# A two-layer hybrid trunk: the instruction queues of VectorE, ScalarE and GpSimd follow the kernel's own planner

## The chip, the cores and the metric

One NeuronCore of a Trainium2 chip. The metric is the device time of one execution in microseconds (us): the median over runs, lower is better. The engines are PE (TensorE, with its weight loads shown as PEld), DVE (VectorE), ACT (ScalarE), POOL (GpSimd) and SP, which only issues DMAs.

## What is computed

Two layers over 512 latent tokens and 256 context tokens of width 1024. In each layer both token sets are normalised and modulated, then projected by one weight `w_in` into three branches and their gates:

```
a: gated DeltaNet, 4 heads of 128, both directions (conv of 4 taps, SiLU, l2 norm of q and k, rotary angles,
   then per block of tokens a triangular solve and a state S <- S*g + k^T u)
b: RG-LRU, 512 channels, both directions (conv, two block-diagonal products, h_t = a_t h_{t-1} + b_t)
c: neighbourhood attention, 4 heads of 128, each query sees an 8x16 window and all context keys
y = sum over branches of sigmoid(gate_i) * (branch_i @ w_branch_i);  x = x + gate * rms_norm(y @ w_out)
```

The last layer returns the latent stream alone.

## The kernel before

Activations lie channel by token. Every f32 weight and activation that feeds a big product is split into two f16 parts (`hi`, `lo`), and a product is three f16 matmuls. `w_in` comes in chunks of 128 output columns (512 KB each); `proj` (line 378) makes one chunk's 24 matmuls of 512 columns and, where the context is wanted, 24 of 256.

**The planner.** The Python program that emits the kernel is itself a small simulator, `Flow` (line 50). Each piece of work is a generator with a rank (0 first, 9 last). `product` (line 121) moves the clock `now` on by the time of a matmul; `note` (line 89) books each DVE, ACT or POOL instruction on its engine with a modelled duration, and keeps when each tile is ready; `until` (line 125) lets a piece wait until its tiles are. `run` (line 65) always resumes the waiting piece of the lowest rank, so the latency-bound pieces (preps rank 1, chains and inverses 2, `pre` 3, attention and RG-LRU cores 4) go first, and the projections (`main`, rank 9) fill PE between them. The order in which instructions are emitted is thus the planner's order.

**Whose order is used.** Only PE's queue follows it: line 31 has `ORDERED = {mybir.EngineType.PE}`, and line 1561 opens `tc.manual_schedule(engines=ORDERED)`. The queues of DVE, ACT, POOL and SP are put in order by the framework, which simulates the program with its own durations and gives each engine the first emitted instruction that is then ready. On the chip each of these queues is worked off in the order in which it was written.

**Stages.** `startup` (504) loads x, forms the modulation and the first h. In a layer, `schedule` (173) lists the projections: the DeltaNet inputs of two heads (half 0) among z gates; then k, q, v of the attention heads, under which the chunks of half 0 run; then half 1 with the fourth attention head; then the gates g of branch 2, the RG-LRU inputs xb with their gates zb, the gates of branches 0 and 1, and the output product with the next layer's h (`out_tiles`, 1405; `out_tail`, 1357).

- `gdn_prep` (969) makes one head's q, k or v: conv of four taps (`conv4`, 687: one ACT and three DVE instructions on 770 columns, tiles `cba` to `coa`), a tanh into a tile `th`, a DVE product, then transposes on PE into PSUM: `pl` holds the four latent tiles and `pc` the two of the context. For k and q, DVE multiplies `pl` by the cosines and by the sines (`rope`), ACT squares each of the six tiles for the norm (`jk`), POOL adds the two halves, `rsqrt` (271) runs eight small dependent DVE instructions (`l6y`, `l6t`, `lr`), DVE scales (`kt` or `qt`), and PE transposes back into a new `pl`, which ACT copies out.
- The tag `cbuf` has two buffers, shared by the conv inputs, `th`, `qt` and `qks` (the q-k products of a half).
- `inverse` (1161) inverts a triangular 128x128 block: `pxt`, then five rounds of `pp`, `px`, `py` on PE, each followed by a DVE or ACT instruction (`ic`, `X`, `di`, `Y`) that the next product needs. `pre` (1092) makes its input, with POOL for `gm`, `dec`, `ll`, `ktl`.
- `Weights.split` (326) turns a landed chunk `raw` into `whi` (ACT) and `wlo` (DVE). `raw` has three buffers, shared with the modulation weights `wm`, the output weights `rwo` and small tables.
- `attn_block` (839) loads its bias table of 256 KB into one buffer when the block begins. The branch `xb` of the layer loads `lw` (256 KB) and splits it before the conv.
- `rg_core` (768): per direction four `lru` products into PSUM, each with a tanh on ACT into `tr` or `ti`, then exponentials, squares and scans.

Of the kernel before, what the change touches and what calls it, by code (L numbers as in the profile page):

```python
# [17 lines left out]
P = 128  # L18
# [12 lines left out]
ORDERED = {mybir.EngineType.PE}  # L31
# [18 lines left out]
class Flow:  # L50
# [4 lines left out]
    def __init__(self):  # L55
        self.now, self.tasks = 0.0, []
        self.free, self.ready, self.used = {}, {}, {}
        self.banks, self.kept, self.wire = [None] * 5, set(), 0.0
# [30 lines left out]
    def note(self, eng, op, args, kw):  # L89
# [3 lines left out]
        start = max([self.free.get(eng, 0.0)] + [self.ready.get(x.name, 0.0) for x in ins])  # L93
        if eng == "act":
            us = n / 1200.0 + 0.09 + 0.09 * sum(isinstance(kw.get(x), bass.AP) for x in ("scale", "bias", "accum_out"))
        elif eng == "pool":
            us = n / 510.0 + 0.1 if op == "tensor_tensor" else n / 1100.0 + 0.12
# [6 lines left out]
        for x in ins:  # L104
            self.used[x.name] = max(self.used.get(x.name, 0.0), end)
        for x in (aps[0], kw.get("accum_out")):
            if x is not None:
                self.ready[x.name] = end + LAT

# [6 lines left out]
    def fetched(self, dst):  # L116

        self.wire = max(self.wire, self.now) + 4 * math.prod(dst.shape) / 357e3
        self.ready[dst.name] = self.wire + FETCH

    def product(self, dst, us):
        self.now += us
        self.ready[dst.name] = self.now + LAT

# [24 lines left out]
    def drop(self, *tiles):  # L149
        self.kept.difference_update(t.name for t in tiles)  # L150

# [47 lines left out]
def build(tc, A, out):  # L199
# [25 lines left out]
    def mm(dst, lhsT, rhs, **kw):  # L225
        n = math.prod(rhs.shape[1:])
        nc.tensor.matmul(dst, lhsT, rhs, **kw)  # L227
        fl.product(dst, max(n, 64) * (4 if rhs.dtype == F32 else 1) / 2400.0)

    def tp(dst, src_, idt):  # L230
        nc.tensor.transpose(dst, src_, idt)  # L231
        fl.product(dst, P * (2 if src_.dtype == F32 else 1) / 2400.0)

    def pair_t(name, wide=True):

        return (plat.tile([P, SEQ], F32, tag="lat", name=name),
                pctx.tile([P, CTX], F32, tag="ctx", name=name + "c") if wide else None)
# [18 lines left out]

    def load_consts():
# [4 lines left out]
        t = wp.tile([P, 5, P], F32, tag="raw", name="tri", bufs=3)  # L262
# [4 lines left out]
    def put_consts(t):  # L267
        V.tensor_copy(C["tri"], t)
        C["cum"], C["sgt"], C["ones"] = C["tri"][:, 0:2], C["tri"][:, 2:4], C["tri"][:, 4]
# [36 lines left out]
    class Weights:  # L306
# [11 lines left out]
        def load(self):  # L318
            if self.seq:
                src_, nk, key = self.seq.pop(0)  # L320
                raw = wp.tile([P, nk, P], F32, tag="raw", name="raw", bufs=3)
                nc.sync.dma_start(raw, src_)
                fl.fetched(raw)
                self.raw.append((raw, nk, key))

        def split(self, pool_=None):
            if self.raw:
                raw, nk, key = self.raw.pop(0)
                kw = {"bufs": 3 if pool_.name == "n0" else 1} if pool_ else {}
# [10 lines left out]
                for k in range(0, nk, step):  # L340
# [3 lines left out]
                    V.scalar_tensor_tensor(lo[:, ks], raw[:, ks], SW, hi[:, ks], op0=OP.mult, op1=OP.subtract)  # L344
                ready.append(True)
# [7 lines left out]
        def ahead(self):  # L353
            self.load()
# [23 lines left out]
    def proj(nk, xs, wide, nm, key, shared=False):  # L378

        w = yield from W.take(key)  # L380
        if shared:
            yield from fl.room(1 + wide)
            o = (pst(nm, [P, SEQ], keep=True), pst(nm + "c", [P, CTX], keep=True) if wide else None)
        else:
            o = pair_t(nm, wide)
        yield from seg(o[0], 0, w, range(nk), nk, xs, 0, SEQ, True)
        if wide:
            yield from seg(o[1], SEQ, w, range(nk), nk, xs, SEQ, NT)
        return o
# [7 lines left out]
    def mod_rows(l, part, fin, load):  # L397
# [5 lines left out]
        for k in range(KD):  # L403
# [5 lines left out]
            fl.product(pm, 0.43)  # L409
# [40 lines left out]
    def wload(l, part, k):  # L450
        raw = wp.tile([P, 2, 512], F32, tag="raw", name="wm", bufs=3)
        nc.sync.dma_start(raw, A["w_mod"][l, part, k])
        return raw

    def gate_rows(l, pp, out_, rowt):
# [4 lines left out]
        def fin(pm):  # L460
# [3 lines left out]
            selg = wp.tile([P, 2, 2, P], F32, tag="raw", name="selg", bufs=3)  # L464
            nc.sync.dma_start(selg, A["selg"])
            g = A["g_post"]
            gp = wp.tile([P, D], F32, tag="raw", name="gp", bufs=3)
# [1205 lines left out]
```

## Time and profile before

| | |
|---|---|
| median of 3 runs | 1741.05 us (1738.36 to 1744.34) |
| the profiled execution's own time | 1741.55 us |
| its span, first to last instruction | 1739.8 us |
| PE busy | 1635.1 us (94%), 11452 matmuls |
| DVE busy | 1168.1 us (67%) |
| ACT busy | 861.1 us (49%) |
| POOL busy | 351.8 us (20%) |
| DMA, mean | 80 GB/s |

Start and end of an instruction are taken from the engine; a matmul's end is modelled, so that overlapping matmuls count as busy once and a short wait can hide under the end of the one before. A wait is idle time of an engine that ended with another engine's signal.

### The profile page before, as it was taken

Reading aid. Unit: us, or ns where it says so; the run is one execution under the profiler, and the core shown is the slowest. Engines: PE = TensorE matmul, PEld = TensorE weight load, DVE = VectorE, ACT = ScalarE, POOL = GpSimd, SP = SyncE. Lnnn points to the kernel's source line nnn. Section 1 sums busy time; section 2 is a strip of 40 time slices with the busy share of each in tenths; the row PEclk is TensorE's granted clock in tenths of the full one; section 3 lists DMA queues with packets and bytes.
Section 4 is the critical chain, followed back from the end, with each engine's and each line's share of the span. In section 5 each row is a group of like instructions: output and inputs, shape, how many; then the busy total and the mean of one; then the engine's idle time right before and its main releaser. Section 6 shows DMA issues by size and latency. Waiting matters only on the chain. (4 is left out here: it accounts for less than half of the span.)

```text
span 1739.8 us, 30312 instructions
## 1 busy us (share of the span) xinstructions
PE 1635.1 (94%) x11452; PEld 1027.8 (59%) x11452; DVE 1168.1 (67%) x2752; ACT 861.1 (49%) x2050; POOL 351.8 (20%) x506
## 2 busy tenths in 40 slices
PE   5999999999999999899999888899999999999998
PEld 4556767766676555455664455577756665544443
DVE  6668777766777556655435756888666888677553
ACT  4445656455545347542432334666454655657341
POOL 0113311002321001231111212323012431012321
PEclk9999999999999999999999999999999999999999
DMA  9211111211222331243432112111121112324432
GB/s 358 59 50 50 44 32 37 67 61 43 86 62 74 122 103 43 79 133 99 134 96 93 36 37 61 43 38 44 55 67 55 44 50 68 122 91 151 139 116 73
DMA packets 48386, 139.79 MB, mean 80 GB/s; under 512 B 8048, under 2 KB 8688, under 8 KB 48240
## 3 DMA queue, kind: packets, MB, share of 16 engines
q1 hardware_dynamic: 48240, 137.86, 24.7%
q8 instruction: 90, 1.47, 0.3%
q14 instruction: 56, 0.46, 0.1%
HBM read 133.64 MB, written 4.19 MB: 79 GB/s over the span
## 5 line engine op out<-in xcount | busy, mean ns | idle before, releaser
L227 PEld LDWEIGHTS <-whi_g 128*128 128x128 f16 x1152 | 109.4, 98 | 88.3 <-issue 11.4
L164 POOL TENSOR_TENSOR gm<-trir,gst 128x256 fp32r<-128x256 f32 x96 | 67.3, 708 | 267.8 <-PE pd L227 261.6
L227 PE MATMUL 1_g<-h,whi_g 128*128 128x512 f16 x384 | 119.2, 383 | 0.2 <-ACT mt L164 0.2
L227 PE MATMUL 0_g<-h,whi_g 128*128 128x512 f16 x384 | 116.6, 379 | 0.0
L227 PE MATMUL py<-wo,mg 128*128 128x512 f16 x480 | 104.9, 379 | 0.0
L227 PEld LDWEIGHTS <-whi_a 128*128 128x128 f16 x704 | 69.5, 99 | 49.2 <-issue 7.8
L164 ACT ACTIVATE X<-px 128x256 f16<-128x256 f32 x181 | 67.6, 382 | 50.4 <-PE px L227 46.1
L164 DVE SCALAR_TENSOR_TENSOR wlo_g<-raw,whi_g 128x512 f16<-128x512 f32 x96 | 68.8, 735 | 33.7 <-ACT whi_g L164 32.5
L164 DVE TENSOR_TENSOR ic<-pp,lmc 128x128 f16<-128x128 f32 x240 | 66.4, 284 | 29.0 <-PE pp L227 26.3
L164 ACT ACTIVATE di<-py 64x128 f16<-64x128 f32 x240 | 63.6, 269 | 44.2 <-PE py L227 24.4
L227 PEld LDWEIGHTS <-whi_b 128*128 128x128 f16 x576 | 54.9, 98 | 45.2 <-issue 10.3
L227 PEld LDWEIGHTS <-wlo_g 128*128 128x128 f16 x576 | 56.4, 98 | 39.4 <-DVE wlo_g L164 0.7
L227 PEld LDWEIGHTS <-mg 128*128 128x128 f16 x480 | 47.0, 98 | 55.1
L164 DVE SCALAR_TENSOR_TENSOR coa<-cba,cva,coa 128x770 f32<-128x770 f32 (+1 forms) x72 | 76.6, 1064 | 4.0 <-ACT coa L164 2.5
L164 ACT ACTIVATE whi_g<-raw 128x512 f16<-128x512 f32 x96 | 58.2, 623 | 37.7 <-DMA raw<-in_w_in 14.9
L227 PE MATMUL 1_g<-h,wlo_g 128*128 128x512 f16 x192 | 73.3, 382 | 0.3 <-DVE wlo_g L164 0.3
L227 PE MATMUL 0_g<-h,wlo_g 128*128 128x512 f16 x192 | 72.8, 379 | 0.0
L227 PEld LDWEIGHTS <-di 128*128 128x128 f16 x480 | 39.5, 98 | 39.0 <-DVE di L164 11.0
L227 PE MATMUL pp<-X,ld 128*128 128x64 f16 x480 | 51.6, 193 | 10.1 <-DVE X L164 4.2
L164 DVE SCALAR_TENSOR_TENSOR wlo_b<-raw,whi_b 128x512 f16<-128x512 f32 x48 | 43.9, 914 | 23.4 <-ACT whi_b L164 22.8
L227 PE MATMUL py<-ident,X 128*128 128x128 f16 x384 | 50.7, 220 | 6.1 <-ACT X L164 3.6
L164 POOL TENSOR_TENSOR mt<-mg,mt 128x768 f32<-128x768 f32 (+1 forms) x16 | 28.9, 1804 | 121.3 <-DVE mt L164 103.3
(658 smaller groups left out, 4745.2 us busy)
## 6 DMA issues: line engine op xcount, KB each, us to landing
raw<-in_w_in SPq DMA_DIRECT2D x128, 512.0 KB, 3.6
wm<-in_w_mod SPq DMA_DIRECT2D x48, 512.0 KB, 4.2
raw<-in_w_branch SPq DMA_DIRECT2D x48, 256.0 KB, 2.7
rwo<-in_w_out SPq DMA_DIRECT2D x16, 512.0 KB, 4.0
xt<-in_xin SPq DMA_DIRECT2D x12, 512.0 KB, 5.0
bias<-in_rpb SPq DMA_DIRECT2D x24, 256.0 KB, 2.7
lw<-in_lru_w SPq DMA_DIRECT2D x8, 256.0 KB, 3.6
x<-xo SPq DMA_DIRECT2D x4, 512.0 KB, 2.9
```

The lines of the kernel that those rows point to most:

```text
L164: return real(*args, **kw)
L227: nc.tensor.matmul(dst, lhsT, rhs, **kw)
```

## The change

All four compute engines are queued in the emitted order, and the planner's model and the emitting pieces are altered with it. The diff has about 660 lines; its core:

```diff
-ORDERED = {mybir.EngineType.PE}
+ORDERED = {mybir.EngineType.PE, mybir.EngineType.DVE, mybir.EngineType.Activation, mybir.EngineType.Pool}
...
     def note(self, eng, op, args, kw):
-        start = max([self.free.get(eng, 0.0)] + [self.ready.get(x.name, 0.0) for x in ins])
+        start = max([self.free.get(eng, 0.0)] + [self.ready.get(x.name, 0.0)
+                                                  - (LAT / 2 if self.near.get(x.name) == eng else 0.0) for x in ins])
+        for x in ins:
+            if x.space == PSUM and self.touch.get(x.name, (eng,))[0] != eng:
+                start = max(start, self.touch[x.name][1] + LAT)
...
-            us = n / 510.0 + 0.1 if op == "tensor_tensor" else n / 1100.0 + 0.12
+            us = (n / 510.0 + 0.1 if n < 512 else n / 375.0) if op == "tensor_tensor" else n / 1000.0 + 0.12
...
-        fl.product(dst, max(n, 64) * (4 if rhs.dtype == F32 else 1) / 2400.0)
+        fl.product(dst, max(n, 70) * 4 / 2400.0 + 0.02 if rhs.dtype == F32 else max(n / 2400.0 + 0.004, 0.035))
...
+    def slot(self):
+        return len(self.ring) < 3 or self.ring[-3] in self.spent
+    def freed(self, *names):
+        for n in names:
+            if n not in self.spent:
+                yield lambda: n in self.spent
+            yield self.used.get(n, 0.0) - self.now
...
         def split(self, pool_=None):
+                if not pool_:
+                    yield fl.until(raw)
...
-            fetch_x(range(TT))
             load_first()
+            fl.fetched(cc)
+            fetch_x(range(TT))
...
         def rg_core(...):
+            yield lambda: sum(xfree) == j
...
+            yield fl.until(lwr)
+            S.activation(lw[0], lwr, AF.Copy, scale=SW)
+            yield fl.until(lw[0])
+            V.scalar_tensor_tensor(lw[1], lwr, SW, lw[0], op0=OP.mult, op1=OP.subtract)
...
+        def load_bias(pp):
+            if tables:
+                hd, i = tables.pop(0)
+                t = pp.tile([P, 512], F32, tag="bias", name="bias", bufs=2)
+                nc.sync.dma_start(t, A["rpb"][l, hd, :, i, :])
+                fl.fetched(t)
+                biases.append(t)
...
         def gdn_prep(...):
-            th = gp.tile([P, NT + 8], F32, tag="cbuf", name="th", bufs=2)
-            S.activation(th[:, :n], c[:, :n], AF.Tanh)
-            V.scalar_tensor_tensor(c[:, :n], th[:, :n], 1.0, c[:, :n], op0=OP.add, op1=OP.mult)
+            S.activation(b[:, :n], c[:, :n], AF.Tanh)
+            V.scalar_tensor_tensor(c[:, :n], b[:, :n], 1.0, c[:, :n], op0=OP.add, op1=OP.mult)
+            cbufs.remove(b.name)
...
-            pl = pst("pl", [P, LT, P], keep=True)
-            pc = pst("pc", [P, 2, P], keep=True) if wide else None
+            banks = [pst(f"pl{i}", [P, cut, P], keep=True) for i in range(2)]
...
-            V.tensor_tensor(dst[:, :LT, :], pl, C["cos"], OP.mult)
-            V.tensor_tensor(tmp ..., pl ..., C["sin"] ..., OP.mult)
-            for t, off in tiles:
-                S.activation(jk, pl[:, t, :] if t < LT else pc[:, t - LT, :], AF.Square, accum_out=ss[:, t:t + 1])
+            for i in (1, 0):
+                for t in range(i * cut, (i + 1) * cut):
+                    S.activation(jk, banks[i][:, t % cut, :], AF.Square, accum_out=ss[:, t:t + 1])
+            for i in range(2):
+                V.tensor_tensor(dst[:, ts, :], src_, C["cos"][:, ts, :], OP.mult)
+                V.tensor_tensor(tmp[:, ts, :] ..., src_ ..., C["sin"][:, ts, :] ..., OP.mult)
...
         def gdn_front(...):
+            yield lambda: len(cbufs) < 2
             b = conv_in(gp, o, "a", 2)
+            cbufs.append(b.name)
```

`near` is the engine that wrote a tile, `touch` the engine that last read a PSUM tile and when. `slot` makes a weight chunk wait for a buffer of the `raw` ring, `freed` a projection for its PSUM tile; `cbufs` counts the users of `cbuf`; `qks` takes its two buffers one by one, the second only when all six preps of the half are spawned and a buffer is free. The first two bias tables are loaded with the first k projection, the next ones each when a block has read its own, into two buffers instead of one; `lw` has two buffers and is loaded one projection earlier. `cut` is three for six tiles and two for four: tiles 0 to 2 go to one PSUM bank, 3 to 5 to the other.

## Rows read from the trace of the kernel before

**Rows 1.** Busy time by stage: stretch, its length, PE, PEld, DVE, ACT, POOL, clock, DMA.

```profile
0.00:43.50 43.50, 24.06 (x197) 17.53 (x197) 26.34 (x87) 21.73 (x48) 3.89 (x9) 0.92 0.94 358
43.50:609.00 565.50, 540.68 (x4357) 379.12 (x4356) 406.67 (x1089) 291.30 (x810) 109.92 (x206) 0.99 0.20 61
609.00:957.00 348.00, 339.44 (x1974) 192.45 (x1973) 187.36 (x272) 145.54 (x228) 62.92 (x35) 0.98 0.30 97
957.00:1044.00 87.00, 74.82 (x521) 42.70 (x519) 55.12 (x162) 28.84 (x70) 20.67 (x38) 0.94 0.11 36
1044.00:1479.00 435.00, 407.13 (x3199) 279.83 (x3200) 338.69 (x915) 248.17 (x701) 104.62 (x185) 0.99 0.17 53
1479.00:1690.00 211.00, 207.52 (x1023) 97.57 (x1022) 135.81 (x175) 119.75 (x177) 43.44 (x29) 1.00 0.40 128
1690.00:1739.80 49.80, 41.40 (x192) 18.59 (x190) 18.15 (x54) 5.80 (x17) 6.33 (x5) 0.96 0.19 64
```

**Rows 2.** Waits of PE, whole span: whom it waited for, us in total, times, longest.

```profile
PE pl L231 <- DVE kt L164: 9.2, 5, 3.7
...
PE xTp L231 <- DVE sq L164: 6.6, 1, 6.6
PE lru L227 <- ACT tr L164: 5.1, 1, 5.1
...
PE pl L231 <- DVE qt L164: 4.1, 3, 2.7
```

**Rows 3.** Busy time in three stretches at a lower granted clock, columns as in rows 1.

```profile
87.14:90.55 3.41, 3.10 (x11) 1.93 (x12) 1.81 (x3) 0.87 (x2) 0.73 (x1) 0.50 0.19 34
...
715.20:722.00 6.80, 4.08 (x12) 1.70 (x12) 3.28 (x5) 5.24 (x9) 0.00 (x0) 0.50 0.17 61
...
1094.10:1097.50 3.40, 3.40 (x16) 1.76 (x16) 3.04 (x6) 0.77 (x2) 1.90 (x3) 0.50 0.53 154
```

**Rows 4.** Timeline of DVE and PE, a k prep of the second layer.

```profile
1031.85 0.16 DVE L164 TENSOR_SCALAR lss<-lss 128x6 f32<-128x6 f32 x1
...
1034.42 1.22 DVE L164 SCALAR_TENSOR_TENSOR wlo_z<-raw,whi_z 128x1024 f16<-128x1024 f32 x1
...
1038.80 0.68 DVE L164 TENSOR_TENSOR kt<-kt,lr 128x512 f32<-128x512 f32 x1
...
1039.54 0.90 PE L231 MATMUL pl<-ident,kt 128*128 128x128 f32 x3 [3.58 <-DVE kt L164]
```

**Rows 5.** Timeline, the first inverses of the second layer.

```profile
1090.85 0.29 DVE L164 TENSOR_TENSOR Y<-lh,lm 128x256 f16<-128x256 f16 x1 [1.39 <-ACT lh L164]
...
1091.74 1.70 DVE L164 SCALAR_TENSOR_TENSOR wlo_v<-raw,whi_v 128x512 f16<-128x512 f32 x2
...
1093.36 0.58 DVE L164 COPY X<-pxt 64x256 f16<-64x256 f16 x2
...
1094.00 0.26 PE L227 MATMUL pp<-X,ld 128*128 128x64 f16 x2 [3.43 <-DVE X L164]
```

**Rows 6.** Timeline of ACT and PE, an RG-LRU core of the first layer.

```profile
715.87 0.63 ACT L164 ACTIVATE whi_g<-raw 128x512 f16<-128x512 f32 x1 [4.54 <-DMA raw<-in_w_in]
...
717.91 0.37 PE L227 MATMUL lru<-xh,lw 128*128 128x256 f16 x1 [5.13 <-ACT tr L164]
```

**Rows 7.** Timeline of the start: one of three small loads of SP, then DVE.

```profile
4.61 0.49 SPq L250 DMA_DIRECT2D ident<-in_ident  x1
...
14.56 0.17 DVE L164 TENSOR_TENSOR xss<-xss 128x4 f32<-128x4 f32 x1 [2.14 <-ACT jk L164]
...
19.12 2.73 DVE L164 TENSOR_SCALAR xt<-xt,xr 128x1024 f32<-128x1024 f32 x4
```

**Rows 8.** Groups: the hop after `pp`, the conv taps and a POOL add (ns min/median/max).

```profile
L164 DVE TENSOR_TENSOR ic<-pp,lmc 128x128 f16<-128x128 f32 x240 | 66.4, 284 | 29.0 <-PE pp L227 26.3
...
L164 DVE SCALAR_TENSOR_TENSOR coa<-cba,cva,coa x72: 733/1021/1959, 64.0 to 1344.5; 128x770 f32<-128x770 f32 x60, 128x512 f32<-128x512 f32 x12
...
L164 POOL TENSOR_TENSOR kt<-kt,rope x8: 1270/1676/2036, 76.5 to 1283.5; 128x512 f32<-128x512 f32 x8
```

More of the change, by code (lines that the diff above doesn't have):

```diff
@@ L56, in __init__ @@
         self.now, self.tasks = 0.0, []
-        self.free, self.ready, self.used = {}, {}, {}
-        self.banks, self.kept, self.wire = [None] * 5, set(), 0.0
+        self.free, self.ready, self.used, self.near = {}, {}, {}, {}
+        self.banks, self.kept, self.wire, self.ring = [None] * 5, set(), 0.0, []
+        self.spent, self.touch, self.sp = set(), {}, 0.0
     def spawn(self, gen, rank, delay=0.0):
@@ L105, in note @@
             self.used[x.name] = max(self.used.get(x.name, 0.0), end)
+            if x.space == PSUM:
+                self.touch[x.name] = (eng, end)
         for x in (aps[0], kw.get("accum_out")):
@@ L382, in proj @@
             yield from fl.room(1 + wide)
-            o = (pst(nm, [P, SEQ], keep=True), pst(nm + "c", [P, CTX], keep=True) if wide else None)
+            lat, ctx = pst(nm, [P, SEQ], keep=True), pst(nm + "c", [P, CTX], keep=True) if wide else None
         else:
-            o = pair_t(nm, wide)
-        yield from seg(o[0], 0, w, range(nk), nk, xs, 0, SEQ, True)
+            yield from fl.freed(*lats[-2:-1])
+            lat, ctx = lat_t(nm), None
+        yield from seg(lat, 0, w, range(nk), nk, xs, 0, SEQ, True)
         if wide:
-            yield from seg(o[1], SEQ, w, range(nk), nk, xs, SEQ, NT)
-        return o
+            if not shared:
+                yield from fl.freed(*ctxs[-1:])
+                ctx = ctx_t(nm)
+            yield from seg(ctx, SEQ, w, range(nk), nk, xs, SEQ, NT)
+        return lat, ctx
     def both(o):
@@ L635, in lru_rates @@
     def lru_rates():
+        yield fl.until(lam)
         V.tensor_scalar(lam, lam, -1.0, None, op0=OP.mult)
@@ L1008, in gdn_prep @@
+            for i in range(2):
+                ts = slice(i * cut, min((i + 1) * cut, LT))
+                src_ = banks[i][:, :ts.stop - ts.start, :]
+                V.tensor_tensor(dst[:, ts, :], src_, C["cos"][:, ts, :], OP.mult)
+                V.tensor_tensor(tmp[:, ts, :].rearrange(sw, two=2, q=32), src_.rearrange(sw, two=2, q=32)[:, :, ::-1, :],
+                                C["sin"][:, ts, :].rearrange(sw, two=2, q=32), OP.mult)
             yield fl.until(tmp)
@@ L1065, in finish @@
                 yield ended(*chains)
+                for t in half["qks"]:
+                    cbufs.remove(t.name)
                 r = small.tile([P, 2, TT], F32, tag="orr", name="orr")
@@ L1118, in pre @@
                             yield lambda: half["used"] >= len(half["kk"]) - 3
+                        if want(s):
+                            slot = half["slots"]
+                            half["slots"] += 1
+                            i = slot // 3
+                            yield lambda: (i < len(half["qks"]) or
+                                           len(cbufs) < 2 and (i == 0 or len(half["preps"]) == 6))
                         yield from fl.room(2)
@@ L1136, in pre @@
                         if want(s):
-                            if "qks" not in half:
-                                half["qks"] = [gp.tile([P, 3, 2, P], F32, tag="cbuf", name="qks", bufs=2)
-                                               for _ in range(2)]
-                            qk = half["qk"][t_] = half["qks"][t_ // 3][:, t_ % 3]
+                            if i == len(half["qks"]):
+                                half["qks"].append(gp.tile([P, 3, 2, P], F32, tag="cbuf", name="qks", bufs=2))
+                                cbufs.append(half["qks"][i].name)
+                            qk = half["qk"][t_] = half["qks"][i][:, slot % 3]
                             S.activation(qk, pqk, AF.Copy)
@@ L1414, in out_tiles @@
                 else:
-                    py = [plat.tile([P, 512], F32, tag="lat", name=f"py{hf}") for hf in range(2)]
+                    yield from fl.freed(*lats[-2:])
+                    py = [lat_t(f"py{hf}") for hf in range(2)]
                 xt = pp.tile([P, D], F32, tag="xt", name="xt", bufs=2)
@@ L1504, in layer @@
                                  o[0].rearrange("p (r n c) -> p r n c", n=4, r=8), AF.Copy, scale=UN * ATT)
+                    fl.drop(*[p for p, _ in both(o)])
                 elif kind == "v":
@@ L1522, in layer @@
                         S.activation(t[:, sl], p, AF.Tanh, scale=0.5 * UN)
+                    fl.drop(*[p for p, _ in both(o)])
                     next(side, None)
```

163 lines of the change are left out of this document (113 added, 50 removed).

## The prediction

> **What bounds the kernel now.** I read the busy time by stage first, since an average hides where PE is full. PE is busy for 540.68 of 565.50 us in the first layer's DeltaNet and attention stage, for 407.13 of 435.00 in the second layer's, for 339.44 of 348.00 between them, and for 24.06 of 43.50 at the start [rows 1]. Its idle time is therefore 19.4 us at the start, 24.8 and 27.9 in the two DeltaNet stages, 8.6 in the first layer's dense part, 12.2 where the layers meet, 3.5 in the second layer's dense part and 8.4 at the end: 104.8 us in all, and nothing that reorders queues can save more than that and what the clock gives back. PE bounds the kernel; the question is only what its waits are made of.
>
> The waits of PE come next. The named ones are k and q preps (9.2 us in 5 waits and 4.1 in 3), one wait of 6.6 for `sq` where the layers meet and one of 5.1 for `tr` in an RG-LRU core [rows 2]. The rest is many short waits in the inverses.
>
> The timelines then say whether a wait is latency or a queue. In the k prep the norm is summed at 1031.85 and `kt` is scaled at 1038.80: 7.0 us for ten small DVE instructions of some 0.16 us, because a `wlo_z` of 1.22 us, conv taps and a softplus stand between them in DVE's queue; PE then waits 3.58 us [rows 4]. In the inverses DVE sat 1.39 us before `Y`, then ran 1.70 us of weight splitting, and only then the copy `X` for which PE waited 3.43 us [rows 5]. In the RG-LRU core ACT sat 4.54 us before a weight split whose chunk had not landed, with the tanh that frees a PSUM bank behind it, and PE waited 5.13 us [rows 6]. All three are the same thing: an instruction that PE needs stands in a queue behind one that is not yet ready or not urgent. The framework ordered these queues by its own simulated times, PE by the planner's, and the two disagree. That is what the change removes.
>
> **The change part by part.** The sum is made against the profiled execution's 1741.55 us, which is 0.5 us above the median of the runs and 1.75 above its span.
>
> *Start.* Three small loads are now issued ahead of x, at some 0.49 us each [rows 7]: x and the squares come 1.5 us later. Against that, the ten small instructions from 14.56 to 19.12 [rows 7] would take about 10 x 0.2 = 2.0 us in a run instead of 4.56: 2.5 us earlier. Net -1.0; ends +1.5 and -2.5.
>
> *k and q preps.* With the norm's instructions in a run the prep of rows 4 is 7.0 - 2.7 = 4.3 us shorter (2.0 for the ten, 0.7 for the scaling), more than the 3.58 that PE waited. The two banks add two DVE instructions to each of 16 preps (about 0.15 us of fixed cost each), and let ACT's squares run beside the DVE reads instead of behind them; both are small beside 4.3. I take 12 of the 13.3 us [rows 2]; ends 0 and 13.3. The cover of the prep is the projection behind it; when a prep is no longer late, the next thing late is its own POOL add.
>
> *Short waits in the inverses, chains and attention.* The two stages hold 52.7 us of idle time [rows 1], 39.4 without the preps' 13.3. Part of it is pure latency (PE to DVE to PE, one `ic` is 284 ns [rows 8]), which no order removes but which the planner can fill with projections; part is the queueing of rows 5. No row splits them. The ends are 0 and 39.4; I take 22, a little over half, since the long ones that I opened are queueing.
>
> *Clock.* After three of the long waits (the longest for `kt`, 3.7 us [rows 2], and those of rows 4 and 5) the granted clock is 0.50, which is 1.2 GHz, for 3.4 us each; PE was busy 3.10 and 3.40 of them in the first and last [rows 3], so each costs about 1.7 us. If the waits go, so do these: -4 of 5; ends 0 and 5.
>
> *RG-LRU.* The split now waits in the planner for its chunk to land, so the tanh goes first: -5.1, and the lowered clock behind it with 4.08 us of PE [rows 3] gives back 2.0. I take -6; ends 0 and -7.
>
> *Where the layers meet.* Idle 12.2 us [rows 1]. The norm chains get shorter, but each now holds DVE for its whole length while DVE also makes h. I take 0, ends +6 and -6 (the `sq` wait of rows 2).
>
> *Biases, `lw`, `cbuf`.* 24 bias loads and 8 of `lw` are issued earlier on SP; DMA is at 0.17 to 0.20 in those stages [rows 1], so they meet nothing. The new wait for a free `cbuf` stands in `main`, so the projections queue behind it; tanh in place takes one user off, and I take 0. Its ends: nothing gained, and a loss of 8 q preps at the mean q wait of 1.4 us [rows 2], 11. SP stays in the framework's order.
>
> *The end* (8.4 us idle) and the dense parts keep their work: 0.
>
> Sum: 1.0 + 12 + 22 + 4 + 6 = 45, so 1741.55 - 45 = **1696.5**, and I say 1696.
>
> **The rivals.**
>
> *Only the long queueing waits go.* If the short waits are latency that the planner already fills as well as it can, their 22 us stay: 1741.55 - 23 = 1718. For it: ahead of `ic` DVE stood idle for 26.3 us until `pp` came [rows 8], and there the hop was prompt. Against it: rows 5. Chance 0.20.
>
> *The shared port.* A POOL add of one size takes 1.27 to 2.04 us and a conv tap 0.73 to 1.96 [rows 8]: something holds one while the other runs. The planner books POOL and DVE as if they were independent, so its order may set more of them side by side. In the two stages POOL is busy 214.5 us, and DVE 745 of 1000.5, so three quarters would already meet by chance; the last quarter is 54 us of DVE, and if half of that reached PE, 27: 1696 + 27 = 1723. Chance 0.08. The Trainium skill, "SBUF — State Buffer", section "Who interferes with whom", states such a rule: a VectorE instruction with two SBUF inputs and a GpSimd instruction that reads SBUF exclude each other for the whole instruction. By that rule the spread of rows 8 is blocking, and the trace agrees with it; the numbers above stand without it.
>
> *Slower: the strict queue holds up the hops.* The planner queues by readiness, not by urgency. A conv tap of 1.02 us (median) emitted just before an `ic` [rows 8] now stays before it on the chip, where the framework could take the `ic` first. The place is the 240 `ic` hops. If one in three waits out a whole tap, 80 x 1.02 = 82 us are added; the gains outside the hops are 23, and a third of the 82 is covered by projections: 1741.55 - 23 + 54 = 1773. It turns the sign when more than 23 / 1.02 = 23 hops of 240, one in ten, are held up uncovered. Against it: the framework's queue has these taps and splits ahead of urgent copies today (rows 4, 5), and the planner's PE order is made with the very same queue in mind. Chance 0.15.
>
> *No change.* The planner's model is off by as much as the framework's, and waits move without shrinking: 1741. Chance 0.07.
>
> **How the numbers follow.** Forecast 0.50, the rivals 0.20, 0.08, 0.15 and 0.07. About 0.3% (5 us) is what a measurement of this kernel can tell from no change. Faster: 0.50 + 0.20 + 0.08 = 0.78; same 0.07; slower 0.15. The low end: taking every term at its better end gives 2.5 + 13.3 + 39.4 + 5 + 7 + 6 = 73, 1668; since modelled matmul ends hide part of each wait, I go to 1660. The high end takes in the no-change case and the start of the slower one, 1744, and leaves out the bulk of the latter. The forecast's own range is 1668 to 1712.
>
> **What would show it.** Right: PE idle in the two DeltaNet stages falls from 52.7 to about 18 us; the waits of `pl` on `kt` and `qt` are nearly gone; the norm's ten DVE instructions stand in a run; no ACT wait for a landing with a tanh behind it; the clock at 87 and 1094 stays at 2.4 GHz; PE busy hardly moves. Wrong: `ic`, `X` or `di` named as the releaser of more PE waits than now, PE waiting for `cba` behind the new gate, longer POOL adds and conv taps, or a wider gap where the layers meet.

## The result, and the profile after

The change made the kernel slower: 1760.99 us (median of 4, 1757.16 to 1763.67) against 1742.69 us of the kernel before in the same session, a ratio of 1.0104 with a 95% interval of 1.0089 to 1.0119. Its profiled execution has a span of 1759.4 us, 19.6 above that of before. (One run of `e5_qt_elsewhere` and two of `e10_pe_split_first`, further down, were disturbed and are left out of their numbers.)

Busy time of the engines over the whole span, before and then after:

```profile
PE 1635.1 (94%) x11452; PEld 1027.8 (59%) x11452; DVE 1168.1 (67%) x2752; ACT 861.1 (49%) x2050; POOL 351.8 (20%) x506
```

```profile
PE 1647.0 (94%) x11452; PEld 1030.7 (59%) x11452; DVE 1190.2 (68%) x2784; ACT 858.1 (49%) x2050; POOL 350.6 (20%) x506
```

Two things are to be read from this pair. PE has the same 11452 matmuls and is busy 11.9 us longer, most of it by a lower clock. The granted clock is 0.979 in the mean, 0.987 before: it stands at 0.50, which is 1.2 GHz, in 15 stretches of 77.0 us together, before in 9 of 47.0. PE is busy for 52.7 and 33.5 us of them, and half the difference, 9.6 us, is an estimate of what that costs. And PE's idle time, span less busy, went from 104.7 to 112.4 us, 7.7 more. The two make the 19.6. DVE too is busy 22.1 us longer, for only 32 more instructions.

Busy time by stage after the change, to be held against [rows 1] (the work stands some 20 us later towards the end, so the last stretch is longer):

```profile
0.00:43.50 43.50, 23.30 (x178) 15.92 (x179) 25.43 (x81) 22.56 (x49) 3.77 (x8) 0.96 0.93 357
43.50:609.00 565.50, 543.81 (x4375) 382.66 (x4374) 400.96 (x1098) 290.22 (x812) 106.49 (x200) 0.99 0.20 60
609.00:957.00 348.00, 345.74 (x2012) 195.80 (x2010) 201.73 (x296) 145.26 (x236) 67.21 (x42) 0.99 0.31 97
957.00:1044.00 87.00, 70.27 (x488) 39.59 (x487) 55.86 (x147) 27.42 (x68) 16.17 (x25) 0.90 0.13 43
1044.00:1479.00 435.00, 405.96 (x3178) 278.31 (x3177) 341.46 (x934) 245.50 (x690) 108.36 (x197) 0.98 0.17 51
1479.00:1690.00 211.00, 197.23 (x950) 91.08 (x949) 136.14 (x165) 114.75 (x168) 37.90 (x26) 0.98 0.39 125
```

PE is fuller in the first layer (543.81 and 345.74 us against 540.68 and 339.44), and emptier from 957 us on: where the layers meet, and in the second layer's dense part, 13.8 us idle against 3.5.

Fixed stretches of time blur what belongs to one piece of work. So here are the lengths between landmarks, the first matmul of a named tile in each trace. The two openings hold the first k and q preparations of a layer; between `q` and `xb` lie the inverses, chains and attention. The last three columns are experiments told below: the change without its gate for q (`e5`), with three faults mended (`e11`), and that with DVE, ACT and POOL free again (`e16`).

| from, to (us) | forecast | before | after | `e5` | `e11` | `e16` |
|---|---|---|---|---|---|---|
| start to `f` | -1 | 33.4 | 32.7 | 32.8 | 31.9 | 33.2 |
| `f` to `0_q` (opening, layer 1) | preps -12 in both | 114.1 | 128.6 | 113.0 | 112.7 | 106.8 |
| `0_q` to `0_xb` | short waits -22 in both layers | 479.0 | 465.2 | 471.8 | 470.9 | 475.6 |
| `0_xb` to output product | -6 | 289.2 | 282.1 | 282.0 | 279.1 | 281.6 |
| to `1_a` (layers meet) | 0 | 101.8 | 104.7 | 104.4 | 105.8 | 102.5 |
| `1_a` to `1_q` (opening, layer 2) | as above | 70.4 | 90.7 | 72.8 | 70.4 | 68.4 |
| `1_q` to `1_xb` | as above | 395.1 | 382.5 | 388.2 | 389.0 | 388.3 |
| `1_xb` to output product | 0 | 206.8 | 222.6 | 223.8 | 213.8 | 208.8 |
| end | 0 | 50.0 | 50.3 | 50.0 | 50.3 | 50.0 |

The loss lies in three places above all: 14.5 and 20.3 us in the openings, 15.8 in the second layer's dense part. Where the layers meet 2.9 more are lost, at the end 0.3; the rest gained.

The waits of PE after the change (whom it waited for; us, times, longest), against [rows 2]:

```profile
PE pl L262 <- DVE qt L195: 14.4, 2, 7.7
PE xTp L262 <- DVE sq L195: 9.7, 1, 9.7
PE pm L467 <- DMA wm<-in_w_mod: 8.5, 5, 2.7
PE pd L258 <- POOL gm L195: 5.6, 11, 1.9
PE 1_a_q L258 <- DVE wlo_a L195: 4.9, 1, 4.9
PE 1_g L258 <- ACT whi_g L195: 4.4, 2, 2.2
PE 1_a_v L258 <- DVE wlo_a L195: 4.4, 2, 2.5
PE pxt L262 <- DVE Y L195: 4.3, 9, 1.2
...
PE 1_g L258 <- DVE wlo_g L195: 3.0, 3, 1.6
PE lru L258 <- ACT tr L195: 2.3, 1, 2.3
...
PE pl L262 <- DVE kt L195: 0.7, 2, 0.4
```

The k preps did what was forecast, 9.2 us to 0.7. The q preps did the opposite, 4.1 to 14.4, in two waits only. And new names stand in the list: `wlo_a`, `whi_g` and `wlo_g`, the two halves of a weight split. Three others grew: the landings of the modulation weights `wm` (2.9 before), and in the inverses POOL's `gm` and DVE's `Y` (1.0 and 1.1 before).

The second of the two q waits, in the timeline of all engines (the first is its twin, 6.75 us at 125.02):

```profile
1062.09 0.27 PE L258 MATMUL 1_a_v_0c<-h,wlo_a 128*128 128x256 f16 x1
...
1062.29 0.28 ACT L195 ACTIVATE jk<-pl 128x128 f16<-128x128 f32 x1 [1.77 <-PE pl L262]
...
1063.90 0.42 DVE L195 TENSOR_TENSOR qt<-pl,cos 128x256 f32<-128x256 f32 x1 [2.66 <-ACT jk L195]
...
1065.48 1.61 POOL L195 TENSOR_TENSOR qt<-qt,rope 128x512 f32<-128x512 f32 x1 [16.73 <-DVE rope L195]
1065.89 1.23 DVE L195 TENSOR_SCALAR lss<-lss 128x4 f32<-128x4 f32 x1
...
1068.55 0.16 DVE L195 SCALAR_TENSOR_TENSOR lr<-l4t,l4y 128x4 f32<-128x4 f32 x1
...
1069.29 0.68 DVE L195 TENSOR_TENSOR qt<-qt,lr 128x512 f32<-128x512 f32 x1
...
1070.03 1.12 PE L262 MATMUL pl<-ident,qt 128*128 128x128 f32 x4 [7.66 <-DVE qt L195]
1070.93 1.06 PE L258 MATMUL 1_z<-h,whi_z 128*128 128x512 f16 x2
```

The preparation is not late. Its norm stands in a run, 1065.89 to 1068.71, as forecast. What is missing is cover: between the last `1_a_v` product and the transposes of `qt` PE's queue holds nothing, and `1_z`, which needs no part of q, comes only after them.

### The profile page after: what moved, and what is told of

It reads as the page before. It is cut to its first block, busy times and chain, and to the rows that moved or that the text cites. A ratio compares the mean times of both kernels' runs of the same rounds, so it can differ in the third digit from the quotient of the medians.

```text
span 1759.4 us, 30281 instructions
## 1 busy us (share of the span) xinstructions
PE 1647.0 (94%) x11452; PEld 1030.7 (59%) x11452; DVE 1190.2 (68%) x2784; ACT 858.1 (49%) x2050; POOL 350.6 (20%) x506
## 5 line engine op out<-in xcount | busy, mean ns | idle before, releaser
L195 ACT ACTIVATE di<-py 64x128 f16<-64x128 f32 x255 | 68.5, 271 | 53.9 <-PE py L258 22.7
L195 DVE SCALAR_TENSOR_TENSOR wlo_g<-raw,whi_g 128x512 f16<-128x512 f32 x96 | 87.2, 933 | 7.0 <-ACT whi_g L195 7.0
L195 ACT ACTIVATE X<-px 128x256 f16<-128x256 f32 x164 | 60.8, 381 | 40.3 <-PE px L258 37.6
L195 DVE SCALAR_TENSOR_TENSOR wlo_b<-raw,whi_b 128x512 f16<-128x512 f32 x48 | 39.6, 825 | 51.9 <-ACT whi_b L195 51.8
L258 PE MATMUL 0_g<-h,wlo_g 128*128 128x512 f16 x192 | 72.8, 379 | 0.0
L195 POOL TENSOR_SCALAR_AFFINE_SELECT dec<-dec 128x256 f32<-128x256 f32 x48 | 22.7, 480 | 223.4 <-ACT dec L195 214.4
L195 ACT ACTIVATE whi_g<-raw 128x512 f16<-128x512 f32 x96 | 56.8, 623 | 20.3 <-DMA raw<-in_w_in 20.2
L195 POOL TENSOR_TENSOR ix<-ix,zz 128x1536 f32<-128x1536 f32 x8 | 27.6, 3449 | 176.0 <-ACT zz L195 176.0
```

The lines of the kernel that those rows point to most:

```text
L195: return real(*args, **kw)
```

## The experiments

**The queues one by one.** The four kernels differ from the change in the set of ordered queues only:

```diff
-ORDERED = {PE, DVE, Activation, Pool}
+ORDERED = {PE}                       # e1_pe_only
+ORDERED = {PE, Activation, Pool}     # e2_dve_free
+ORDERED = {PE, DVE}                  # e3_pe_dve
+ORDERED = {PE, DVE, Pool}            # e4_act_free
```

`e1_pe_only`:

> The changed kernel with one line put back: only PE follows the planner's order, DVE, ACT and POOL are ordered by the framework again; the new planner model, gates, banks and early biases stay. Theory A (the strict queues cost, the rest of the change gains): well under 1760, at or below the kernel before, 1720 to 1743, with the waits of PE for wlo_a, qt and sq shorter. Rival B (the planner's new model and gates cost, by another PE order): 1755 or more, as with the queues. Rival C (the two add up): about 1750.

`e2_dve_free`:

> The changed kernel with DVE alone ordered by the framework; PE, ACT and POOL follow the planner. Theory A in the form that DVE's queue is the one that costs: as fast as with PE alone ordered, within 5 us. Rival (ACT's queue costs, tanh and copies behind a wait for PE): no faster than 1755.

`e3_pe_dve`:

> The changed kernel with PE and DVE in the planner's order, ACT and POOL by the framework. If DVE's queue costs: 1755 to 1765, like the change. If ACT's or POOL's queue costs: like PE alone, 1720 to 1743.

`e4_act_free`:

> The changed kernel with ACT alone ordered by the framework; PE, DVE and POOL follow the planner. If ACT's queue costs (it stood 8.4 us behind a transposed copy with a tanh behind that): 1745 or less. If DVE's queue costs: 1755 to 1765.

Measured: 1746.99 us (ratio to before 1.0022, 1.0010 to 1.0033), 1759.27 (1.0087), 1773.44 (1.0174) and 1780.66 (1.0211, 1.0196 to 1.0226). Freeing all three queues gives back 14 us, and the kernel still isn't faster than before, nearest to the third expectation; freeing one or two of them gives 2 us or costs 12 and 20. `e3_pe_dve` and `e4_act_free` lie above every range expected, and why is not shown. The change missed the forecast by 64 us, so the larger part of that lies outside the new queues, and an order of half the queues is no way between.

**The gate on `cbuf`.** A q preparation no longer takes a `cbuf`, its rotated tile goes to `oa`, which isn't in use yet:

```diff
             else:
-                yield lambda: len(cbufs) < 2
-                dst = gp.tile([P, TT, P], F32, tag="cbuf", name="qt", bufs=2)
-                cbufs.append(dst.name)
+                dst = half["oa"][:, hl]
...
-            if which == "q":
-                cbufs.remove(dst.name)
```

> The changed kernel with the rotated q of a prep written into the half's output tile, which is idle until the chains run, instead of the shared conv buffers; it no longer counts against the gate that holds back the next projection. Theory A (in the opening of a layer PE waits for qt because the gate keeps the projections from being queued ahead of its transposes): the waits of pl on qt, 14.4 us in 2, fall below 4, and the time by 8 to 20 us, to 1741 to 1753. Rival B (qt is late by DVE's and ACT's strict queues alone, the gate only names it): the waits move to another tile of the prep and the time stays at 1756 to 1763.

Measured: 1740.92 us, ratio 0.9983 (0.9970 to 0.9996), 20 us faster than the change. Both openings are back at 113.0 and 72.8 us; of the 33.5 us that they gain, 12.3 are lost again between `q` and `xb`, since side work that the long openings had done is now done there (30 and 28 matmuls move). Of the 20.6 us between the two profiled runs 9.0 are idle time of PE (112.4 to 103.4), and 11.6 are busy time for the same matmuls (1647.0 to 1635.4). PE's wait for q, which was expected to fall below 4:

```profile
PE pl L262 <- DVE oa L195: 8.2, 5, 3.6
```

Is it the gate or the buffer? The next kernel puts the tile in `oa` too, but still counts it as a holder of a `cbuf`:

```diff
+                yield lambda: len(cbufs) < 2
                 dst = half["oa"][:, hl]
+                cbufs.append(f"qt{hl}")
```

> The change as it is, with q's rotated tile in `oa` as in the run that put it elsewhere (1740.9), but with the planner still counting q as a holder of a `cbuf` and still gating on it, though no buffer is taken. Theory 1: the cost of some 20 us is the gate itself, by which the planner holds the main path's next projections and q's own rotation until a buffer is counted free: this kernel stays at 1757 to 1763, with PE's wait of `pl` for q's tile near the 14.4 us of the change. Rival: the cost is the buffer, that is the hardware wait for the tile's earlier reader; then the kernel goes with the run that put q elsewhere: 1739 to 1744.

Measured: 1755.92 us, ratio 1.0070 (1.0052 to 1.0087), with the wait back:

```profile
PE pl L262 <- DVE oa L195: 20.4, 6, 7.8
```

It is the gate, for 15 of the 20 us: PE's idle time is back, 114.9 us, and what is still missing lies in its busy time, 1638.2 against 1647.0 in the change. No instruction waits for a buffer here; the planner, told that both are held until q's transposes are done, holds `main` in front of the next conv input, and so plans no projection before them. PE obeys the plan. The edit brings back two gates, q's own and that of the conv input; that the second one drains PE is read from the program and the timeline, and the two were not separated. (The time is 1.1 us under the range expected.)

The same edit on the kernel before, which has no gate:

> The kernel before, with one edit: q's rotated tile lies in its half's `oa` instead of one of the two `cbuf` buffers. Nothing else of the change is in it. Theory 1, what the first four runs suggest: the gate that the change adds is its dear part, and the change without gate and with only the tensor engine queued in order (1725.7) gains 17 us over before by its other parts. Then this edit alone changes the kernel before little: it had no gate, and its q preparations cost it 4.1 us of waits in three cases; 1738 to 1745. Rival: two `cbuf` buffers for th, q and the conv inputs are what binds in both kernels, and the whole gain belongs to the third place for q: then this kernel comes to 1726 to 1732 and the change's other parts are worth nothing. The opening from the last product of the modulation to the end of layer 1's last q (114.1 us before, 110.0 with the tensor engine alone in order and q elsewhere) would then be 110 or less here.

Measured: 1745.91 us, ratio 1.0007 (0.9996 to 1.0018). The place of the tile is worth nothing by itself. And the edit of `e5` with only PE ordered, `ORDERED = {PE}`:

> PE alone in the planner's order, as in the first experiment (1747), with q in the output tile. Theory A (the gate costs with either queue order): 1727 to 1741, below the kernel before. Rival B: 1744 to 1750, as without the edit.

Measured: 1725.74 us, ratio 0.9904 (0.9883 to 0.9924), 21 us under `e1_pe_only`. The gate costs the same, 20 or 21 us, in either order.

**The rank of the weight split.** In the change the second layer's dense part waits for `whi_g`. The timeline of ACT and PE there:

```profile
1669.74 1.06 ACT L195 ACTIVATE wo<-rwo 128x1024 f16<-128x1024 f32 x1 [4.25 <-DMA rwo<-in_w_out]
1670.70 1.13 ACT L195 ACTIVATE whi_g<-raw 128x512 f16<-128x512 f32 x2
...
1671.37 0.60 PE L258 MATMUL 1_g<-h,whi_g 128*128 128x512 f16 x2 [2.16 <-ACT whi_g L195]
```

ACT stood 4.25 us before a split of the output weights whose chunk had not landed, and `whi_g`, for which PE waited, stood behind it: the situation of [rows 6], now made by the planner, which gives weight splits rank 7, the last before `main`'s 9. The edit:

```diff
-            fl.spawn(self.split(), 7, 0.3)
+            fl.spawn(self.split(), 0, 0.3)
```

> The changed kernel with the splitting of landed weight chunks at rank 0 instead of 7. Theory A (in a strict queue work of the lowest rank comes last whenever there is a burst, and PE then waits for its weights): the waits for wlo_a, wlo_g, wlo_b, whi_g (some 20 us) fall to under 8 and those for wm landings (8.5 us) shrink since the ring turns faster; 1740 to 1753. Rival B (the splits now hold up the hops of the inverses): those waits go but others in the inverses come, 1757 to 1770.

> Both edits, q in the output tile and splits first. If the two causes are separate: the sum of the two gains, 1722 to 1745. If they are one (a late prep by whichever way): no better than the better of the two.

Measured: alone 1747.82 us, ratio 1.0032 (1.0019 to 1.0045), 13 us faster than the change; with the tile in `oa` 1730.88, ratio 0.9940 (0.9920 to 0.9960), 10 faster than `e5_qt_elsewhere`. The two gains add, but for 3 us. The dense part falls from 222.6 to 213.0 and 214.0, and PE's waits for `whi_g` and `wlo_g` are gone from the list; those for `wlo_a` in the openings stay (11.2 us in the change, 11.0 with the edit), so that the sum under 8 that was expected is missed. The rest of the dense part's loss, 6 to 7 us, goes with another wait: PE waits there for landings of `wm`, 1.1 us before, 6.9 in the change and 7.1 with the edit, which was expected to shorten these waits. Why `wm` lands late is not shown. With free queues the rank should be worth nothing:

> Only the tensor engine's queue in the planner's order, q's rotated tile in `oa`, no gate for it, and the task that splits a weight at the planner's first rank instead of its last. Theory 1: the split's rank matters only where the vector engine works strictly in the planner's order, since a free queue there is ordered by what is ready; then the rank adds nothing here: 1722 to 1729. Rival: the rank matters because it sets where the split stands in the program in either case; then the 10 to 13 us of the strict kernel appear again: 1712 to 1716, the last dense part of layer 2 shorter by 5 or more.

Measured: 1722.81 and 1723.22 us, ratio 0.9876 (0.9856 to 0.9895) beside 0.9904 without the edit; the intervals overlap, so no more than a few us, as expected.

**The softplus in one run.** At the second opening of the changed kernel, DVE and PE:

```profile
1027.02 1.66 DVE L195 SCALAR_TENSOR_TENSOR spp<-spp,spq 128x48 f32<-128x48 f32 x7
...
1027.99 0.59 PE L258 MATMUL 1_a_q<-h,whi_a 128*128 128x512 f16 x2
...
1031.60 0.68 DVE L195 TENSOR_TENSOR kt<-kt,lr 128x512 f32<-128x512 f32 x1
1032.20 1.22 DVE L195 SCALAR_TENSOR_TENSOR wlo_a<-raw,whi_a 128x1024 f16<-128x1024 f32 x1
...
1033.48 0.61 PE L258 MATMUL 1_a_q<-h,wlo_a 128*128 128x512 f16 x1 [4.89 <-DVE wlo_a L195]
```

A task that issues its softplus without handing back to the planner puts all of it into the queue at once; `wlo_a` waits behind steps that nobody is waiting for. On top of `e7_both`:

```diff
         V.reciprocal(s, s)
+        yield fl.until(s)
         V.tensor_tensor(s, s, w, OP.mult)
...
         for k in (15, 13, 11, 9, 7, 5, 3):
+            yield fl.until(p)
             V.scalar_tensor_tensor(p, p, 1.0 / k, q, op0=OP.add, op1=OP.mult)
```

> All four queues in order, q's rotated tile in `oa`, split at the first rank (1730.9), and in the softplus of the decays the planner is asked after each of some ten small vector steps instead of none, so that other work can stand between them. Theory: the run of some twenty small vector steps stands in front of wlo_a in the strict queue, and the two waits of PE for wlo_a at the opening of layer 2 (4.9 and part of 6.4 us) come from it; spread, 1721 to 1727, with the 4.9 us wait of 1_a_q for wlo_a under 1.5. Rival: PE's waits for wlo_a come from the raw buffer being filled late or from ACT's half of the split, and the burst only fills the vector engine's slack: 1729 to 1733 with the same wait.

Measured: 1723.86 us, ratio 0.9880 (0.9865 to 0.9896), 7 faster than `e7_both`, and the wait of `1_a_q` is gone from the list; that of `1_a_v`, of which a part was expected to go too, stays (6.4 and 6.8 us). This is the change with three faults mended: 20 us under before. Then the three queues free again, `ORDERED = {PE}`:

> The strict kernel with all three edits (q in `oa`, split at the first rank, softplus spread; 1723.9) with the vector, scalar and pool queues free again. If the strict queues themselves, freed of the three faults, give what the prediction took from them (22 us of short waits), this kernel is 15 us or more slower than that: 1739 or more. If a queue in the planner's order is worth nothing beside one that takes what is ready, as the run with two edits suggests (1722.8), it comes to 1720 to 1726.

Measured: 1717.89 us, ratio 0.9860 (0.9842 to 0.9879), under both ranges expected, the fastest kernel of all and 6 us under the strict one. So over the whole kernel the strict order of DVE, ACT and POOL is worth nothing here, even with its faults mended.

By stretches it is worth something, and loses more. Four pairs of kernels differ in these three queues alone: the change and `e1`, `e5` and `e8`, `e7` and `e10`, `e11` and `e16`. In each pair the strict kernel is shorter from `0_q` to `0_xb` (by 4.7 to 10.7 us) and from there to the output product (2.4 to 4.5), and longer in the openings (2.0 to 5.8 and 1.9 to 10.2), where the layers meet (1.7 to 4.0) and in the second layer's dense part (5.0 to 13.2). Each of these is one profiled run.

The softplus edit also gains with the queues free: by the medians `e16` is 5 us under `e10`, which lacks it (the intervals overlap), though `1_a_q` doesn't wait for `wlo_a` in `e10`. How much of its 7 us in the strict kernel is the burst in DVE's queue, and how much another order of PE, is open.

In `e16` PE is busy 1631.4 us of 1715.2, so idle for 83.8 against 104.7 before:

```profile
PE xTp L262 <- DVE sq L195: 6.6, 1, 6.6
PE pl L262 <- DVE kt L195: 6.0, 4, 2.5
...
PE pl L262 <- DVE oa L195: 3.0, 3, 1.7
```

**Where the gain comes from.** The two banks put back to one of 512 and one of 256, in `e10_pe_split_first`:

> Only the tensor engine's queue in order, q in `oa`, split at the first rank (1722.8), and the transposed tiles of a preparation back in one bank of 512 and one of 256, with the rope products ahead of the squares, as before the change. What is left of the change are the planner's durations and landings, the ring of raw buffers, the biases and the lru weights ahead. Theory A, the prediction's step for the preparations (12 us): the two banks shorten the path from transposes to rotated tile; undone, 1731 to 1737, PE's waits of `pl` for kt and oa back at 10 or more. Theory B: the gain of 21 us over before lies in the planner's better knowledge, which places PE's own order, and the banks are worth little: 1720 to 1727.

Measured: 1732.58 us, ratio 0.9946 (0.9924 to 0.9967): the banks, with the order of reads that goes with them, are worth 10 us there, and the waits of `pl` for kt and oa come to 13.5 us (7.1 with them). What else the change has (durations, landings, the ring, early loads), together with q in `oa` and the split first, holds this kernel 11 us under before; it was not taken apart. The banks alone on the kernel before:

> The kernel before with one part of the change alone: a preparation's transposed tiles in two banks of equal halves, the squares of the second bank first, the rope products after them. Theory A (the banks carry the preparations' 12 us): 1731 to 1736, PE's waits of `pl` for kt and qt, 13.3 us before, at 4 or less. Theory B (the gain needs the planner's knowledge): 1741 to 1748.

Measured: 1767.52 us, ratio 1.0142 (1.0122 to 1.0162): the same edit costs 24 us, which neither theory had. Waits of PE, and the k prep that answers to [rows 4]:

```profile
PE pl L231 <- DVE kt L164: 15.2, 5, 5.9
...
PE pl L231 <- DVE qt L164: 7.4, 3, 4.1
```

```profile
1039.84 0.26 ACT L164 ACTIVATE jk<-pl 128x128 f16<-128x128 f32 x1
...
1042.36 0.23 DVE L164 TENSOR_TENSOR kt<-pl,cos 128x128 f32<-128x128 f32 x1
...
1045.13 0.17 DVE L164 TENSOR_SCALAR lss<-lss 128x6 f32<-128x6 f32 x1
...
1053.18 0.68 DVE L164 TENSOR_TENSOR kt<-kt,lr 128x512 f32<-128x512 f32 x1
...
1053.91 1.11 PE L231 MATMUL pl<-ident,kt 128*128 128x128 f32 x4 [5.05 <-DVE kt L164]
```

The products of the rotation now come after the squares of their bank, 2.5 us after the first square, with other work of ACT between the squares. The old planner knows nothing of that, thinks both run at once, and puts the transposes into PE's order too early. The planner's new rule, that a bank has one reading engine at a time, is three lines of the change:

```diff
+        for x in ins:
+            if x.space == PSUM and self.touch.get(x.name, (eng,))[0] != eng:
+                start = max(start, self.touch[x.name][1] + LAT)
```

Added to the banks on the kernel before, and taken from the fastest kernel:

> The kernel before with the two banks alone (1767.5, 24 us slower than before) and one piece of the planner's new knowledge: a PSUM bank has one reading engine at a time, so a reader on another engine starts when the last one has ended. If that piece is what the banks lacked, the planner queues the transposes of kt and q later and the waits of `pl` for kt and qt (22.6 us in eight cases) fall below 14: 1738 to 1750. If the loss has another cause (the longer chain of squares and products itself), it stays at 1760 to 1770.

> The fastest kernel so far (only the tensor engine in order, q in `oa`, split first, softplus spread; 1717.9) without the planner's rule of one reader to a bank. If that rule carries the banks' gain, this kernel loses 10 us or more: 1728 to 1745, with waits of `pl` for kt and oa of 15 us or more (9.0 now). If the other additions (durations, landings, the ring) carry it, 1715 to 1723.

Measured: 1754.25 us (ratio 1.0072, 1.0049 to 1.0095), 13 of the 24 us back, a little less than expected; and 1778.37 us (1.0210, 1.0185 to 1.0235), 60 us slower than with the rule, more than twice what was expected. In the first the waits of `pl` for kt and qt fall from 22.6 to 6.2 us, below the 13.3 of before, and the openings are back (111.4 and 69.3 us; 124.6 and 80.1 without the rule). What still separates it from before lies elsewhere, from `0_q` to `0_xb` above all (492.5 against 479.0), and is open. In the second PE is idle for 123.8 us (83.8 with the rule) and busy 20.0 longer. Its waits:

```profile
PE pl L259 <- DVE kt L192: 20.6, 7, 5.8
PE pl L259 <- DVE oa L192: 20.5, 7, 5.6
```

Three lines that add no instruction and touch only the planner's clock decide over 60 us, since PE's order is made from that clock. The kernel before with all its queues ordered was not tried, nor a third `cbuf`.

## Why the prediction was wrong

The forecast was 1696.5 us, and 1760.99 were measured, 64 more. Three things to which it gave no cost, the gate, the rank of the split and the softplus, are 37 of them (down to 1723.86, `e11`). The other 27 are gains that it had too large, as the rows of `e11` show: the openings give 1.4 us where the preps were to give 12, the stretches between `q` and `xb` 14.2 of 22, and where the layers meet and in the second dense part 4.0 and 7.0 are lost.

*Biases, `lw`, `cbuf`: the step that failed.* It took 0 with a loss of 11 as its end, at 8 q preps times the mean q wait of 1.4 us. The gate cost 20 us (`e5`, `e8`, `e12`). The step did say that the gate stands in `main` and that the projections queue behind it; it then priced the wait that the trace had, with cover, and not a preparation whose cover the gate takes away. A whole q prep without cover is 6.75 and 7.66 us of PE, and there is one such to a layer. In idle time the end of 11 was about right: between the profiled runs of the change and `e5` it is 9.0, of `e6` and `e7` 10.9, of `e1` and `e8` 14.5. As much again is PE's busy time, 11.6, 14.9 and 10.9 us, for which the step had no term; the stretches at 0.50 account for some 5, 13 and 8.5 of it (half of what PE is busy in them, an estimate). The step also had the earlier loads meet nothing; PE's waits for `wm` grew by 5.6 us, and whether by these loads is not shown.

*k and q preps, -12.* For k the step held: 8.5 of 9.2 us went. For q the gate above it made 14.4 of 4.1. The two banks, "small beside 4.3", are not small: +10 us if undone (`e14`), and -24 if done without the planner's new rule (`e15`). The step had the squares "run beside the DVE reads instead of behind them": in the change none of the 64 products of a rotation overlaps a square, since the strict queues do all squares first (DVE idle for 2.66 us at 1063.90); with the queues free 23 of 64 do (`e16`). The norm in a run gained a few us at most: the waits of `pl` for kt and q's tile are 5.4 us with it (`e11`) and 9.0 without (`e16`), and the run itself takes 2.8 us in the timeline above where 2.0 were reckoned, 1.23 of them its first instruction (see the last section).

*Short waits, -22.* Between `q` and `xb` the two layers gained 26.4 us together, which looks like the forecast met; but with the gate gone it is 14.1, and with the queues free (`e16`) still 10.2. In the four pairs that differ in the queues alone the strict order gives 3.7 to 13.1 of the 22 in these stretches, and over the whole kernel it costs 6 to 15 us. The reason given, that "the framework ordered these queues by its own simulated times, PE by the planner's, and the two disagree", doesn't carry the gain: the mended kernels gain with the framework's order too, and more, because their planner's times mend PE's order, as `e18` shows for one part of them.

*RG-LRU, -6.* The number held, 7.1 us, the terms by half: the wait for `tr` gave 2.8 of its 5.1 (5.1 to 2.3), and the clock still stands at 0.50 for 3.41 us in that stretch. The rest came from waits that the step didn't name, above all for `yb` and `cbb`, 3.4 us before and none after. That part is luck. *Start, -1.* Held: -0.7.

*The end and the dense parts, 0.* The second layer's dense part lost 15.8 us. The larger part has the mechanism of the slower rival, an urgent instruction behind one that isn't, but not at the place given: not a conv tap before `ic` on DVE, but the output weights' split before `whi_g` on ACT, where the split has rank 7. Moved to rank 0, 9.6 us of it come back (`e6`); the rest goes with the waits for `wm`. The rival's own place stayed clean: PE's waits for `ic` went from 3.2 us to 1.2. Beside it they grew, by 3.2 for `Y` and 4.6 for `gm`.

*Layers meet, 0.* 2.9 us worse, within the ends given: the wait for `sq` from 6.6 to 9.7. It is 9.7 or 9.8 in the strict kernels `e5`, `e7` and `e11`, and 6.5 or 6.6 in `e1`, `e8`, `e10` and `e16` with free queues, so it comes from the strict order, and from DVE's: with DVE alone free (`e2`) it is 6.8, with only PE and DVE ordered (`e3`) 10.5. Whether the norm chains in a run do it was not tried.

*Clock, -4.* It went the other way. In each of three long waits, the two for q and that for `sq`, PE stood idle for 6.75 to 9.75 us, and the clock is at 0.50 from within the wait to past its end:

```profile
121.14:127.97 6.83, 2.95 (x10) 1.88 (x11) 4.45 (x13) 1.80 (x5) 0.37 (x4) 0.50 0.00 0
1066.63:1073.46 6.83, 3.43 (x10) 1.75 (x11) 4.10 (x13) 2.28 (x5) 0.63 (x4) 0.50 0.00 0
977.88:988.12 10.24, 4.00 (x12) 2.04 (x13) 7.07 (x18) 2.60 (x6) 3.75 (x3) 0.50 0.00 0
```

PE is busy 11.9 us more for the same matmuls, some 9.6 of it by the clock. With the faults mended and the queues free (`e16`) it is busy 3.7 us less than before, and in stretches at 0.50 for 24.8 us instead of 33.5; half the difference, some 4 us, is the -4 of the forecast, once its waits are gone. In the strict kernel mended (`e11`) PE is busy 3.3 us less, but still in such stretches for 32.5 us, so that little of this is the clock.

*The shared port.* It is there, see below, but not as the bound (and the conv tap of 0.73 us from which the rival reckoned is one of the twelve on 512 columns; one on 770 takes 1.02): the strict kernel of 1723.9 us has DVE busy for 1207.1 us, the free one of 1717.9 for 1169.7, and the whole difference between them is 6 us.

## What to carry to other kernels

A gate in a planner is paid where the queue behind it runs dry: price it by the whole latency of what it waits for, without cover, not by the wait that the old trace shows, and add what PE loses behind it by a lowered clock, here some 5 to 13 us. A planner that issues PE's order is worth what its clock knows of dependences; three lines of such knowledge were worth 60 us in one kernel and 13 in another, and a rearrangement made without them cost 24. Putting further engines into the planner's order makes its ranks and its uninterrupted runs of instructions binding, so each of them must be looked at first; here the framework's order of those engines was better by 6 to 15 us.

## What was not expected of the hardware

The weight splits of the gates on DVE got longer without being changed. Their group before, and after (duration in ns min/median/max):

```profile
L164 DVE SCALAR_TENSOR_TENSOR wlo_g<-raw,whi_g x96: 664/684/2195, 414.8 to 1680.0; 128x512 f16<-128x512 f32 x96
```

```profile
L195 DVE SCALAR_TENSOR_TENSOR wlo_g<-raw,whi_g x96: 658/683/3572, 421.4 to 1696.3; 128x512 f16<-128x512 f32 x96
```

The median stays at 0.68 us and the longest goes from 2.2 to 3.6. Sorted by whether a POOL instruction runs at the same time, the 55 of after that have none beside them take 0.68 us in the mean, the 41 that have one 1.27; before, 16 of 96 had one. This is 18 of DVE's additional 22 us. It agrees with the rule that the prediction cited from the Trainium skill, "SBUF — State Buffer", section "Who interferes with whom"; what a strict order adds is that it brings such pairs together: 41 and 52 in the strict kernels (after, `e11`), 16 and 15 in those with free queues (before, `e16`).

A small instruction with one input is held up too. The first of a norm, `TENSOR_SCALAR lss`, takes 0.16 to 0.17 us in all 16 preps before, with no POOL instruction beside it. After, seven of the 16 take 1.23 to 1.43 us, and six of these end 0.03 us after the POOL add of their own preparation does, as at 1065.89 above (1067.12 and 1067.09).
